# Five layer-norm boundaries: the next stage's first slab multiplied block by block, the slabs after it copied later on ScalarE

## The chip, the cores and the metric

The kernel runs on one core of a Trainium2 chip. The metric is the device time of one execution in microseconds (us). TensorE multiplies matrices, VectorE and ScalarE work on elements, GpSimd does a few small operations, and SyncE issues most transfers. The time before is the median of three runs, 965.1 us (963.51 to 965.26).

## The reference

Three transformer blocks in a row on one sequence of 256 positions and 1024 features, all in float32. Cut to what matters:

```python
# block 1
x = layer_norm(2**.25 * x + concat(stick_breaking_attention, memory_attention) @ w_out)
x = layer_norm(2**.25 * x + square(relu(x @ w_up)) @ w_down)         # 4096 wide
# block 2, layer 0
x = layer_norm(4**.25 * x + mla_mixer(x))     # low-rank q and kv, 8 heads with rotary parts
x = layer_norm(4**.25 * x + conv_ffn(x))      # (silu(g) * a) @ w_down, a and g by a 3-tap convolution
# block 2, layer 1
x = layer_norm(4**.25 * x + hyena_mixer(x))   # gated long convolutions through Fourier transforms
x = layer_norm(4**.25 * x + conv_ffn(x))
```

There are six layer norms. Five of them are followed by another stage; these five places are called boundaries here, numbered in order of time: into the first feed-forward network (FF1), into the latent attention (MLA), into the first convolution FFN, into Hyena, into the second convolution FFN.

## The kernel before, in words

**Numbers in two parts.** To reach float32 accuracy with the fast reduced type (F32R), each operand is split in a high part (a copy on ScalarE, line 67) and a low part (source minus high on VectorE, line 68). A product is three matmuls: high x high, low x high, high x low.

**Slabs.** Weights come from memory in slabs of 128 x 1024 (512 KB). `weights()` takes one of three raw buffers (`wraw`), loads it through SyncE's queue (line 82), and splits it into one of five pairs `whi`, `wlo` (pool `wspl`). A raw buffer is free again when the low part is done.

**Activations.** `x` is kept feature by feature: 8 tiles of 128 features, high and low, 256 positions in two blocks of 128 rows. `gemm_b` (line 102) multiplies a slab by x over all 256 positions, 24 matmuls of 256 columns; `gemm_wide` (lines 110 and 112), used in FF1, takes high and low x side by side, 8 matmuls of 512 columns and 8 of 256.

**A boundary** is written in `Down.end`. The down projection's last four slabs are kept back (`tail`), and in program order there follow: the tail of block 0 (12 x 2 matmuls of 512 columns); `ln_block(0)`, the norm of rows 0 to 127; the loads of the next stage's four first slabs (`w_up_f` and the like); the tail of block 1; `first_mm(0)`, 24 matmuls of 512 columns (line 199) that use block 0 of x as weights and give the next stage's first 512 outputs, position by position, copied to `utok` by ScalarE (line 201); `ln_block(1)`; `first_mm(1)`.

`ln_block` runs lines 159 to 170 on VectorE (one power on GpSimd, line 165), then eight 128x128 transposes on TensorE (line 178, tile `ln_t`), four to a bank, and splits each bank into x: high on ScalarE, low on VectorE. After the boundary the stage begins with its next slab, called the lead slab here: `ff1_mm(4)` in FF1, `c_mm(4)` in MLA, `mm(0)` in the convolution FFNs, `hy_mm(4)` in Hyena. Then come transposes of `utok` (line 209, tile `f4t`) and further slabs.

**Order.** The framework orders each engine's instructions when the program is built: of those it takes to be ready by its own estimate, the one that stands first in the program goes first. `tc.issue_after(ins)` adds one rule: what the block issues on the engine of `ins` goes behind `ins` in that engine's order. Before, it is used with `norm["inst"]`, the last VectorE instruction of the norm: `ln_block(1)` goes behind block 0's, and the low parts of the six slabs after a boundary (`norm["after"] = 6`) go behind block 1's. Their high copies on ScalarE have no such rule.

**Positions.** `rope_tables`, called in FF1 at `i == 3`, loads the positions and a small table through SyncE's queue, and VectorE and ScalarE make sine and cosine from them for the MLA stage.

Of the kernel before, what the change touches and what calls it, by code (L numbers as in the profile page):

```python
# [9 lines left out]
F32 = mybir.dt.float32  # L10
F32R = mybir.dt.float32r
# [32 lines left out]
def block_kernel(ctx, tc, A, out, taps=None):  # L44
# [21 lines left out]
    def split(hi, lo, src):  # L66
        nc.scalar.activation(hi, src, AF.Copy)  # L67
        nc.vector.tensor_tensor(lo, src, hi.bitcast(F32), op=ALU.subtract)  # L68
# [7 lines left out]
    def weights(ap, dst=None, dma=False):  # L76


        n = ap.shape[-1]
        raw = raw_tile()  # L80
        hi, lo = dst or [wspl.tile([P, 1024], F32R, name=t, tag=t) for t in ("whi", "wlo")]
        norm["load"] = nc.sync.dma_start(raw[:, :n], ap)
        if dma:
            nc.scalar.activation(hi[:, :n], raw[:, :n], AF.Copy)
            nc.scalar.activation(lo[:, :n], raw[:, :n], AF.Copy, scale=-1.0)
            nc.gpsimd.dma_start(lo[:, :n], ap, accum_op=ALU.add)
            return hi, lo
        with ExitStack() as es:
            if norm["after"] > 0:
                norm["after"] -= 1  # L90
                es.enter_context(tc.issue_after(norm["inst"].ins))
            split(hi[:, :n], lo[:, :n], raw[:, :n])
        return hi, lo
# [59 lines left out]
    def ln_block(b, acc, x, gb, alpha, last):  # L153
# [15 lines left out]
        for h, sl in enumerate(halves):  # L169
            norm["inst"] = nc.vector.scalar_tensor_tensor(s[:, sl], s[:, sl], rs, bb[:, sl],  # L170
                                                          op0=ALU.mult, op1=ALU.add)
            if last:
                nc.sync.dma_start(out[b * P:(b + 1) * P, sl], s[:, sl])
                continue
            ps = bank("ln_t")
            for k in range(4):
                kk = 4 * h + k
                nc.tensor.transpose(ps[:, k * P:(k + 1) * P], s[:, kk * P:(kk + 1) * P], ident)
            pv = ps.rearrange("p (k t) -> p k t", k=4)
            kb = (slice(None), slice(4 * h, 4 * h + 4), slice(b * P, (b + 1) * P))  # L180
            split(x[0][kb], x[1][kb], pv)
# [6 lines left out]
    def first_mm(b, x, ws, utok):  # L188
# [12 lines left out]
        nc.scalar.activation(utok[:, b, :], ps, AF.Copy)  # L201

# [11 lines left out]
    class Down:  # L214
# [24 lines left out]
        def end(self, gb, alpha, first, room=None):  # L239
            last = first is None  # L240
            x = utok = ws = None
# [5 lines left out]
            if not last:  # L247
                room = room or [None] * 4
                ws = [weights(first[i], room[i]) for i in range(4)]
            self.tail(1)  # L250
            if not last:
                first_mm(0, x, ws, utok)
            with tc.issue_after(norm["inst"].ins):
                ln_block(1, self.acc, x, gb, alpha, last)
            if not last:
                first_mm(1, x, ws, utok)
                norm["after"] = 6
            return x, utok
# [259 lines left out]
    x, utok = dn.end(gb, ALPHA_1, A["w_up_f"], spare(p1, F4_TAGS))  # L518
# [32 lines left out]
    def rope_tables():  # L551
        posi = p2.tile([P, S], I32, name="posi")
        pp = A["positions"]
        nc.sync.dma_start(posi, bass.AP(tensor=pp.tensor, offset=pp.offset, ap=[[0, P], [1, S]]))
        invf = p2.tile([P, 2], F32, name="invf")
        nc.sync.dma_start(invf, A["c_rope"])
# [40 lines left out]
    ready = [ff1_act(ff1_mm(4))]  # L597
# [12 lines left out]
    x, utok = dn.end(gb, ALPHA_1, A["mla_w_in_f"], spare(p2, F4_TAGS))  # L610
# [35 lines left out]
    c4 = c_mm(4)  # L646
# [131 lines left out]
    x, utok = dn.end(gb, ALPHA_2, A["ffn_w_up_f"][0], spare(p3, F4_TAGS))  # L778
# [88 lines left out]
    def conv_ffn(layer, x, utok, nxt, side):  # L867
        with ExitStack() as es:
# [28 lines left out]
            ready = [up(2)]  # L897
# [9 lines left out]
            return dn.end(gb, ALPHA_2, nxt)  # L907

    x, utok = conv_ffn(0, x, utok, A["hy_w_in_f"], hyena_filter)
# [137 lines left out]
    va = [hy_mm(4)]  # L1047
# [44 lines left out]
    x, utok = dn.end(gb, ALPHA_2, A["ffn_w_up_f"][1], [(room[:, i, 0], room[:, i, 1]) for i in range(4)])  # L1092
# [3 lines left out]
    conv_ffn(1, x, utok, None, None)  # L1096
# [117 lines left out]
```

## Time and profile before

| | before |
|---|---|
| median of three runs | 965.1 us |
| the profiled execution's own time | 964.65 us |
| its span (first to last instruction) | 962.9 us |
| granted TensorE clock, mean over the span | 0.992 |
| busy share TensorE / VectorE / ScalarE / GpSimd | 97% / 79% / 56% / 7% |
| bytes moved by transfers | 173.83 MB, mean 181 GB/s |

A row of the timeline gives start, duration, engine, line, operation, tiles (out<-in), shape and count; like instructions that follow each other are merged, so the duration of a merged row runs from the first one's start to the last one's end. In square brackets stands how long the engine was idle before, and who ended that. PE is TensorE, PEld its weight loads, DVE VectorE, ACT ScalarE, POOL GpSimd, SP SyncE; a "q" behind the name is the engine's sequencer. Matmuls overlap, so a row's mean duration is longer than the distance from one to the next. A row of a stretch (windows) gives its start and end, length, busy time and count of each engine, granted clock, transfer share and GB/s.

### The profile page before, as it was taken

Reading aid. Unit: us, or ns where it says so; the run is one execution under the profiler, and the core shown is the slowest. Engines: PE = TensorE matmul, PEld = TensorE weight load, DVE = VectorE, ACT = ScalarE, POOL = GpSimd, SP = SyncE. Lnnn points to the kernel's source line nnn. Section 1 sums busy time; section 2 is a strip of 40 time slices with the busy share of each in tenths; the row PEclk is TensorE's granted clock in tenths of the full one; section 3 lists DMA queues with packets and bytes.
Section 4 is the critical chain, followed back from the end, with each engine's and each line's share of the span. In section 5 each row is a group of like instructions: output and inputs, shape, how many; then the busy total and the mean of one; then the engine's idle time right before and its main releaser. Section 6 shows DMA issues by size and latency. Waiting matters only on the chain.

```text
span 962.9 us, 15208 instructions
## 1 busy us (share of the span) xinstructions
PE 932.9 (97%) x5808; PEld 823.7 (86%) x5808; DVE 761.1 (79%) x1201; ACT 539.9 (56%) x878; POOL 64.0 (7%) x61
## 2 busy tenths in 40 slices
PE   9999999999999999999999999998989999999996
PEld 6889788888887898788899999888978799999995
DVE  6887679777667879779889788889779878777776
ACT  4676636454445577556666566445675355555551
POOL 0000000000000010011312211001210000000000
PEclk9999999999999999999999999999989999999999
DMA  7764536655665443576555556436995565555551
GB/s 248 261 198 132 166 117 223 204 175 181 192 193 193 160 126 109 176 248 220 184 170 177 176 182 198 153 98 159 262 242 144 173 231 184 181 192 185 186 177 44
DMA packets 51082, 173.83 MB, mean 181 GB/s; under 512 B 6236, under 2 KB 7101, under 8 KB 50881
## 3 DMA queue, kind: packets, MB, share of 16 engines
q1 hardware_dynamic: 48656, 164.34, 52.6%
q0 software_dynamic: 2352, 8.52, 4.6%
q8 instruction: 46, 0.75, 0.3%
q14 instruction: 28, 0.22, 0.1%
HBM read 171.13 MB, written 1.05 MB: 179 GB/s over the span
## 4 chain that ended last, share of the span: by engine, by line
PE 75%; DVE 11%; DMA 7%; ACT 4%; issue 2%; SPq 0%; DVEq 0%; ACTq 0%; POOLq 0%
PE up L102 23%; PE acc L116 9%; PE acc L117 9%; PE acc L118 9%; PE up L110 5%; PE f L199 5%; DVE wlo L68 3%; PE up L112 3%; PE proj L102 2%; DMA wraw<-w_v 1%; ACT whi L67 1%; DMA wraw<-hy_w_in 1%; DMA wraw<-ffn_w_up_f 1%; PE hin L102 1%; DMA wraw<-w_qk 1%
## 5 line engine op out<-in xcount | busy, mean ns | idle before, releaser
L68 DVE TENSOR_TENSOR wlo<-wraw,whi 128x1024 fp32r<-128x1024 f32 (+1 forms) x255 | 310.4, 1220 | 78.4 <-ACT whi L67 77.5
L67 ACT ACTIVATE whi<-wraw 128x1024 fp32r<-128x1024 f32 (+1 forms) x255 | 265.2, 1044 | 128.1 <-PE acc L117 45.8
L102 PE MATMUL up<-x,whi 128*128 128x256 f32 x1280 | 173.7, 283 | 2.0 <-DVE t L790 2.0
L102 PEld LDWEIGHTS up<-x,whi 128*128 128x128 f32 x1280 | 164.8, 191 | 6.2 <-ACT whi L67 2.1
L118 PE MATMUL acc<-wlo,hh 128*128 128x512 f32 x304 | 119.9, 396 | 0.0
L116 PE MATMUL acc<-whi,hh 128*128 128x512 f32 x304 | 119.9, 396 | 0.0
L117 PE MATMUL acc<-whi,hl 128*128 128x512 f32 x304 | 119.9, 395 | 0.0
L102 PE MATMUL up<-x,wlo 128*128 128x256 f32 x640 | 89.8, 283 | 0.0
L787 ACT ACTIVATE t<-up,wc 128x256 f32<-128x256 f32 x80 | 37.7, 473 | 91.8 <-PE up L102 89.0
L102 PEld LDWEIGHTS up<-x,wlo 128*128 128x128 f32 x640 | 82.4, 192 | 0.0
L788 DVE SCALAR_TENSOR_TENSOR t<-up,wc,t 128x255 f32<-128x255 f32 x80 | 38.2, 479 | 46.3 <-ACT t L787 46.0
L118 PEld LDWEIGHTS acc<-wlo,hh 128*128 128x128 f32 x304 | 57.1, 188 | 13.5
L116 PEld LDWEIGHTS acc<-whi,hh 128*128 128x128 f32 x304 | 57.4, 189 | 11.3 <-ACT hh L67 0.5
L117 PEld LDWEIGHTS acc<-whi,hl 128*128 128x128 f32 x304 | 57.0, 188 | 11.0 <-DVE hl L68 0.3
L110 PE MATMUL up<-x,whi 128*128 128x512 f32 x224 | 56.6, 395 | 0.0
L165 POOL TENSOR_TENSOR ln_rs<-ln_rs,mhalf 128x1 f32<-128x1 f32 x12 | 11.5, 958 | 646.3 <-DVE ln_rs L164 646.3
L110 PEld LDWEIGHTS up<-x,whi 128*128 128x128 f32 x224 | 41.8, 188 | 10.6 <-issue 1.1
L102 PE MATMUL hin<-x,whi 128*128 128x256 f32 x320 | 46.7, 292 | 0.0
L102 PEld LDWEIGHTS hin<-x,whi 128*128 128x128 f32 x320 | 42.7, 199 | 0.3
L790 DVE SCALAR_TENSOR_TENSOR t<-up,wc,t 128x255 f32<-128x255 f32 x80 | 38.3, 480 | 2.1
L67 ACT ACTIVATE hh<-h 128x256 fp32r<-128x256 f32 x32 | 13.1, 415 | 39.1 <-DVE h L544 38.0
L112 PEld LDWEIGHTS up<-x,wlo 128*128 128x128 f32 x224 | 30.6, 190 | 2.3
(404 smaller groups left out, 1665.2 us busy)
## 6 DMA issues: line engine op xcount, KB each, us to landing
wraw<-ffn_w_up SPq DMA_DIRECT2D x80, 512.0 KB, 4.2
wraw<-ffn_w_down SPq DMA_DIRECT2D x44, 512.0 KB, 3.7
wraw<-w_down SPq DMA_DIRECT2D x32, 512.0 KB, 3.5
wraw<-w_up SPq DMA_DIRECT2D x28, 512.0 KB, 4.3
wraw<-hy_w_in SPq DMA_DIRECT2D x20, 512.0 KB, 5.1
wraw<-w_qk SPq DMA_DIRECT2D x14, 512.0 KB, 4.5
wlo<-hy_w_in POOLq DMA_DIRECT2D x11, 512.0 KB, 9.4
wraw<-w_out SPq DMA_DIRECT2D x8, 512.0 KB, 3.4
```

Of the source, the lines that this page charges most:

```text
L67: nc.scalar.activation(hi, src, AF.Copy)
L68: nc.vector.tensor_tensor(lo, src, hi.bitcast(F32), op=ALU.subtract)
L102: nc.tensor.matmul(ps, a[:, off + k * P:off + (k + 1) * P], m[:, k, :], start=i == 0, stop=i == len(seq) - 1)
L110: nc.tensor.matmul(ps, wh[:, k * P:(k + 1) * P], xx[:, k], start=k == 0, stop=False)
L112: nc.tensor.matmul(ps[:, :S], wl[:, k * P:(k + 1) * P], xh[:, k, :], start=False, stop=k == KT - 1)
L116: nc.tensor.matmul(ps, ah, mh, start=start, stop=False)
L117: nc.tensor.matmul(ps, al, mh, start=False, stop=False)
L118: nc.tensor.matmul(ps, ah, ml, start=False, stop=stop)
L199: nc.tensor.matmul(ps, x[xi][:, k, tb], ws[k // 2][wi][:, o:o + 512], start=i == 0, stop=i == len(seq) - 1)
L787: norm["act"] = nc.scalar.activation(dst, ps, AF.Copy, scale=w3[:, 1:2])
L788: nc.vector.scalar_tensor_tensor(dst[:, 1:], ps[:, :S - 1], w3[:, 0:1], dst[:, 1:], op0=ALU.mult, op1=ALU.add)
L790: norm["dve"] = nc.vector.scalar_tensor_tensor(dst[:, :S - 1], ps[:, 1:S], w3[:, 2:3], dst[:, :S - 1], op0=ALU.mult, op1=ALU.add)
```

## The change

The lead slab moves into `Down.end`. Its load and its high copy stand behind the four first slabs; the high copy goes behind block 0's last high split of x on ScalarE (`norm["x"]`). `lead_mm(0)`, 16 matmuls of 128 columns (high weights by high and by low x of block 0), stands behind `first_mm(0)` and ahead of `ln_block(1)`. Behind `first_mm(1)` stand the low part (VectorE, after block 1's norm), `lead_mm(1)`, 16 more, and 8 matmuls of 256 columns with the low weights. The results gather in one PSUM bank, an accumulator bank of the down projection where the first slabs have room of their own (boundaries 1, 2, 3 and 5), else a bank of the common pool. In FF1 the lead is no longer in the wide form, so its activation takes the Relu path of `ff1_act`.

The next five slabs' high copies on ScalarE now go behind block 1's last high split of x, as their low parts already went behind block 1's norm. The positions and their table are loaded through GpSimd's queue.

```diff
     def split(hi, lo, src):
-        nc.scalar.activation(hi, src, AF.Copy)
-        nc.vector.tensor_tensor(lo, src, hi.bitcast(F32), op=ALU.subtract)
+        return (nc.scalar.activation(hi, src, AF.Copy),
+                nc.vector.tensor_tensor(lo, src, hi.bitcast(F32), op=ALU.subtract))
...
             if norm["after"] > 0:
                 norm["after"] -= 1
                 es.enter_context(tc.issue_after(norm["inst"].ins))
+                es.enter_context(tc.issue_after(norm["x"].ins))
             split(hi[:, :n], lo[:, :n], raw[:, :n])
...
-            split(x[0][kb], x[1][kb], pv)
+            norm["x"] = split(x[0][kb], x[1][kb], pv)[0]
...
+    def lead_mm(ps, b, x, hi):
+
+        tb = slice(b * P, (b + 1) * P)
+        for j in range(2):
+            for k in range(KT):
+                nc.tensor.matmul(ps[:, tb], hi[:, k * P:(k + 1) * P], x[j][:, k, tb],
+                                 start=(b, j, k) == (0, 0, 0), stop=False)
...
-        def end(self, gb, alpha, first, room=None):
+        def end(self, gb, alpha, first, lead=None, room=None):
...
                 ws = [weights(first[i], room[i]) for i in range(4)]
+                raw = raw_tile()
+                lw = [wspl.tile([P, 1024], F32R, name=t, tag=t) for t in ("whi", "wlo")]
+                nc.sync.dma_start(raw, lead)
+                with tc.issue_after(norm["x"].ins):
+                    nc.scalar.activation(lw[0], raw, AF.Copy)
             self.tail(1)
             if not last:
+                ps = bank("lead") if room[0] is None else acc_bank(0, 0, "lead")
                 first_mm(0, x, ws, utok)
+                lead_mm(ps, 0, x, lw[0])
             with tc.issue_after(norm["inst"].ins):
                 ln_block(1, self.acc, x, gb, alpha, last)
             if not last:
                 first_mm(1, x, ws, utok)
-                norm["after"] = 6
-            return x, utok
+                with tc.issue_after(norm["inst"].ins):
+                    nc.vector.tensor_tensor(lw[1], raw, lw[0].bitcast(F32), op=ALU.subtract)
+                lead_mm(ps, 1, x, lw[0])
+                ps = ps[:, :S]
+                for k in range(KT):
+                    nc.tensor.matmul(ps, lw[1][:, k * P:(k + 1) * P], x[0][:, k, :], start=False, stop=k == KT - 1)
+                norm["after"] = 5
+            return x, utok, ps
...
-        nc.sync.dma_start(posi, bass.AP(tensor=pp.tensor, offset=pp.offset, ap=[[0, P], [1, S]]))
+        nc.gpsimd.dma_start(posi, bass.AP(tensor=pp.tensor, offset=pp.offset, ap=[[0, P], [1, S]]))
         invf = p2.tile([P, 2], F32, name="invf")
-        nc.sync.dma_start(invf, A["c_rope"])
+        nc.gpsimd.dma_start(invf, A["c_rope"])
...
-    ready = [ff1_act(ff1_mm(4))]
+    ready = [ff1_act(lead)]
...
-    c4 = c_mm(4)
...
-            ready = [up(2)]
+            ready = [act(2, [lead, mm(1)])]
...
-    va = [hy_mm(4)]
+    va = [lead]
```

The calls of `dn.end` pass the lead slab (`A["w_up"][0]`, `A["mla_w_in"][0]`, `A["ffn_w_up"][0, 0]`, `A["hy_w_in"][0]`, `A["ffn_w_up"][1, 0]`) and hand its result on.

More of the change, by code (lines that the diff above doesn't have):

```diff
@@ L237, in tail @@
                     gemm_a(self.acc, b, h, act, w, False, i == len(self.pend) - 1)
-        def end(self, gb, alpha, first, room=None):
+        def end(self, gb, alpha, first, lead=None, room=None):
             last = first is None
-            x = utok = ws = None
+            x = utok = ws = lw = ps = None
             self.tail(0)
@@ L517, in block_kernel @@
         u_dn(k)
-    x, utok = dn.end(gb, ALPHA_1, A["w_up_f"], spare(p1, F4_TAGS))
+    x, utok, lead = dn.end(gb, ALPHA_1, A["w_up_f"], A["w_up"][0], spare(p1, F4_TAGS))
     ph.close()
@@ L609, in block_kernel @@
             next(mlp, None)
-    x, utok = dn.end(gb, ALPHA_1, A["mla_w_in_f"], spare(p2, F4_TAGS))
+    x, utok, c4 = dn.end(gb, ALPHA_1, A["mla_w_in_f"], A["mla_w_in"][0], spare(p2, F4_TAGS))
     ph.close()
@@ L777, in block_kernel @@
         u_wo(k)
-    x, utok = dn.end(gb, ALPHA_2, A["ffn_w_up_f"][0], spare(p3, F4_TAGS))
+    x, utok, lead = dn.end(gb, ALPHA_2, A["ffn_w_up_f"][0], A["ffn_w_up"][0, 0], spare(p3, F4_TAGS))
     ph.close()
@@ L864, in hyena_filter, with conv_ffn @@
         return steps + [(load_dft, "c_inv1"), (load_dft, "c_inv2")]
-    def conv_ffn(layer, x, utok, nxt, side):
+    def conv_ffn(layer, x, utok, lead, nxt, nxt_lead, side):
         with ExitStack() as es:
@@ L906, in conv_ffn @@
                         f(*a)
-            return dn.end(gb, ALPHA_2, nxt)
-    x, utok = conv_ffn(0, x, utok, A["hy_w_in_f"], hyena_filter)
+            return dn.end(gb, ALPHA_2, nxt, nxt_lead)
+    x, utok, lead = conv_ffn(0, x, utok, lead, A["hy_w_in_f"], A["hy_w_in"][0], hyena_filter)
     tap("t_l0")
@@ L1091, in block_kernel @@
     room = keep.tile([P, 4, 2, D], F32R, name="Kf", tag="Kf")
-    x, utok = dn.end(gb, ALPHA_2, A["ffn_w_up_f"][1], [(room[:, i, 0], room[:, i, 1]) for i in range(4)])
+    x, utok, lead = dn.end(gb, ALPHA_2, A["ffn_w_up_f"][1], A["ffn_w_up"][1, 0], [(room[:, i, 0], room[:, i, 1]) for i in range(4)])
     ph.close()
     tap("t_hy")
-    conv_ffn(1, x, utok, None, None)
+    conv_ffn(1, x, utok, lead, None, None, None)
 def _tiles(w):
```

## The prediction

> **What bounds the kernel now.** I read the page's busy shares and chain first, then TensorE's waits, then the five layer-norm boundaries stretch by stretch, and last their timelines. Durations come from the profiled execution, which took 964.65 us (span 962.9); the median of the runs shown, 965.1, is 0.45 us above it.
>
> ```profile
> span 962.9 us, 15208 instructions
> PE 932.9 (97%) x5808; PEld 823.7 (86%) x5808; DVE 761.1 (79%) x1201; ACT 539.9 (56%) x878; POOL 64.0 (7%) x61
> PE 75%; DVE 11%; DMA 7%; ACT 4%; issue 2%; SPq 0%; DVEq 0%; ACTq 0%; POOLq 0%
> ```
>
> TensorE is busy 97% of the span and holds three quarters of the chain. So work added to TensorE is time added, unless it falls into one of TensorE's idle stretches, and the question is how much idle time the boundaries have. TensorE's waits by releaser (total us, times, longest):
>
> ```profile
> PE hin L102 <- DMA wlo<-hy_w_in: 3.7, 4, 1.8
> PE y L116 <- DVE g L790: 2.7, 2, 2.2
> PE hyt L935 <- DVE u L790: 2.6, 1, 2.6
> ...
> PE up L102 <- DVE t L790: 2.0, 2, 1.8
> ...
> PE f L199 <- ACT x L67: 0.9, 3, 0.3
> ```
>
> The last row is the wait that the change aims at: first_mm (L199) for the copy of the normalised rows. It is 0.9 us in the whole program. The other rows lie inside later stages (Hyena, first convolution FFN). The five boundaries, each from the end of the down projection's tail into the lead slab (window, length, then busy us of TensorE, weight loads, VectorE, ScalarE, GpSimd):
>
> ```profile
> 128.40:144.20 15.80, 15.50 (x76) 12.71 (x75) 12.20 (x17) 5.08 (x8) 0.99 (x1) 1.00 0.36 124
> 314.00:330.00 16.00, 15.94 (x85) 13.02 (x84) 13.58 (x23) 6.08 (x15) 0.92 (x1) 1.00 0.33 105
> 406.50:422.20 15.70, 15.40 (x82) 12.97 (x81) 12.39 (x17) 4.39 (x7) 0.93 (x1) 1.00 0.43 130
> 619.00:637.00 18.00, 16.10 (x85) 12.90 (x84) 13.95 (x20) 7.45 (x10) 0.99 (x1) 1.00 0.40 124
> 757.00:781.00 24.00, 23.64 (x123) 19.37 (x123) 19.46 (x30) 9.23 (x13) 1.91 (x2) 1.00 0.43 154
> ```
>
> TensorE is idle 0.30, 0.06, 0.30, 1.90 and 0.36 us there: only the fourth boundary (into Hyena) has a hole worth filling. The third (into the first convolution FFN) stands for the others; TensorE, then ScalarE, then VectorE:
>
> ```profile
> 410.49 2.03 PE L199 MATMUL f<-f4h,x 128*128 128x512 f32 x8
> 412.36 1.03 PE L178 MATMUL ln_t<-ident,xt 128*128 128x128 f32 x8
> 413.70 1.21 PE L199 MATMUL f<-f4h,x 128*128 128x512 f32 x4 [0.30 <-ACT x L67]
> ...
> 419.32 1.12 PE L102 MATMUL up<-x,whi 128*128 128x256 f32 x8
> ...
> 421.24 2.08 PE L102 MATMUL up<-x,whi 128*128 128x256 f32 x16
> ```
>
> ```profile
> 412.56 0.60 ACT L201 ACTIVATE utok<-f 128x512 f32<-128x512 f32 x1 [5.85 <-PE f L199]
> 413.05 1.08 ACT L67 ACTIVATE x<-ln_t 128x512 fp32r<-128x512 f32 x2
> ```
>
> ```profile
> 410.53 1.41 DVE L170 SCALAR_TENSOR_TENSOR xt<-xt,ln_rs,ln_b 128x512 f32<-128x512 f32 x2
> ```
>
> Block 1's norm ends on VectorE at 411.94, before first_mm(0) ends, so the transposes start at 412.36 with no wait. They are issued by 412.36 + 8 x 0.109 = 413.23; block 1's first matmul starts at 413.70, a hole of 0.47 us.
>
> **Paces.** A merged row gives the pace as (its time less one duration) / (count less one). 128x512: (2.03 - 0.40) / 7 = 0.233 us. 128x256: (2.08 - 0.28) / 15 = 0.120. 128x128 transposes: (1.03 - 0.27) / 7 = 0.109. (0.40, 0.28 and 0.27 are the single durations of those shapes.)
>
> **The lead slab's matmuls.** Before, the lead slab costs 24 matmuls of 256 columns, 24 x 0.120 = 2.88 us; at the first boundary it is the wide form (8 of 512, 8 of 256), and takes 144.02 - 141.21 = 2.81:
>
> ```profile
> 141.21 2.01 PE L110 MATMUL up<-x,whi 128*128 128x512 f32 x8
> ...
> 144.02 1.03 PE L209 MATMUL f4t<-ident,utok 128*128 128x128 f32 x8
> ```
>
> After, it is 2 x 16 of 128 columns and 8 of 256: half the columns in each of the 32, but each loads its own 128x128 weights. No row of before has such a matmul on the reduced type. From below, weights with a single moving column; from above, plain f32 at 256 columns:
>
> ```profile
> 338.07 0.51 PE L667 MATMUL ss<-ones,sq 128*128 128x1 f32 x4
> ```
>
> ```profile
> 394.12 1.13 PE L760 MATMUL o<-sm_pt,v_mla 128*128 128x256 f32 x4 [0.74 <-ACT sm_pt L294]
> ```
>
> These give (0.51 - 0.25) / 3 = 0.087 and (1.13 - 0.39) / 3 = 0.248. I take 0.109, the transposes: nearest in shape (128 weight columns, 128 moving), and the first row says that the weights alone cost nearly that. The 0.120 of the 256-column rows is the likely slow end. New lead: 32 x 0.109 + 8 x 0.120 = 4.45 us. That is +1.64 at the first boundary and +1.57 at each of the second, third and fifth.
>
> The row for weights says a 128-column matmul can't halve the 256-column one. [...]
>
> **Fourth boundary.** TensorE, ScalarE and VectorE:
>
> ```profile
> 623.06 2.00 PE L199 MATMUL f<-whi,x 128*128 128x512 f32 x8
> 625.74 0.44 PE L209 MATMUL f4t<-ident,utok 128*128 128x128 f32 x2 [0.69 <-ACT utok L201]
> 627.30 1.38 PE L178 MATMUL ln_t<-ident,xt 128*128 128x128 f32 x8 [1.12 <-DVE xt L170]
> ```
>
> ```profile
> 622.58 1.06 ACT L67 ACTIVATE whi<-wraw 128x1024 fp32r<-128x1024 f32 x1 [2.44 <-DMA wraw<-hy_w_in]
> ```
>
> ```profile
> 626.50 1.41 DVE L170 SCALAR_TENSOR_TENSOR xt<-xt,ln_rs,ln_b 128x512 f32<-128x512 f32 x2
> ```
>
> first_mm(0) is issued by 623.06 + 8 x 0.23 = 624.9, and the transposes wait for the norm until 627.30: 2.4 us with 0.2 of work in them. The lead's high copy ends at 623.6, so lead_mm(0), 16 x 0.109 = 1.74, fits in wholly. What is left after block 1 is 1.74 + 0.96 = 2.70 against 2.88: -0.18. The late thing is then still block 1's norm.
>
> **Order at the other four.** lead_mm(0) stands ahead of ln_block(1) in the program, and the transposes are ready when first_mm(0) ends, so it goes ahead of them: it pushes transposes, copy and first_mm(1) back by 1.74 us and fills no hole. What it does save: utok's copy is off ScalarE by then. The first four transposes end at 412.36 + 3 x 0.109 + 0.27 = 412.96, and the copy started at 413.05: 0.09 saved at boundaries one and three, about 0.10 at the fifth, where the rows wait for VectorE instead, nothing at the second: -0.28. The fifth boundary, where the transposes run into VectorE's end but the hole is the same, 771.57 - (770.23 + 8 x 0.109) = 0.47:
>
> ```profile
> 770.23 1.33 PE L178 MATMUL ln_t<-ident,xt 128*128 128x128 f32 x8
> 771.57 5.87 PE L199 MATMUL f<-Kf,x 128*128 128x512 f32 x24
> ```
>
> **Copies held back on ScalarE.** Five slabs' high copies now wait for block 1's high split. At the first boundary (ScalarE, VectorE):
>
> ```profile
> 125.43 2.01 ACT L67 ACTIVATE whi<-wraw 128x1024 fp32r<-128x1024 f32 x2 [5.14 <-PE acc L117]
> ...
> 134.89 1.08 ACT L67 ACTIVATE x<-ln_t 128x512 fp32r<-128x512 f32 x2
> ```
>
> ```profile
> 133.56 2.35 DVE L68 TENSOR_TENSOR wlo<-wraw,whi 128x1024 fp32r<-128x1024 f32 x2
> ```
>
> The two copies of 125.43 move behind the split, which ends near 137.6 (135.97 + 1.74 - 0.09): the second slab is copied by 138.7 and subtracted by 139.9. It is needed after the lead and the eight transposes of 144.02, at about 146.4: cost nothing, slack 6 us. Its raw buffer is freed 4 to 5 us later than before (133.56 + 2.35 = 135.9), so the load into it lands near 139.9 + 3.5 = 143.4 instead of 139.4, and three slabs of 2.8 us each stand before its use:
>
> ```profile
> wraw<-w_down SPq DMA_DIRECT2D x32, 512.0 KB, 3.5
> ```
>
> Queued behind the held copies on ScalarE: utok's copy and the activations, all after first_mm(1). Without that slack a slab costs 1.06 + 1.22 us of ScalarE and VectorE time in the open. The lead's high copy waits for block 0's split, over 5 us before its use. The low part after the norm was so before. The loads keep their order on SyncE.
>
> **Positions on GpSimd's queue.** Two small DMAs leave SyncE's queue, for a queue with nothing in it (GpSimd):
>
> ```profile
> 310.89 0.99 POOL L165 TENSOR_TENSOR ln_rs<-ln_rs,mhalf 128x1 f32<-128x1 f32 x1 [178.82 <-DVE ln_rs L164]
> ```
>
> They can only go earlier; GpSimd's next work is 179 us away. VectorE loses a wait under a TensorE-bound stage: 0. If they landed late, VectorE's conversion would hold the splits queued behind it, with several slabs ahead as cover. The lead's activation in the first FFN (Relu and one multiply instead of three operations) and the accumulator bank borrowed for the lead: 0, both end before that bank's first use.
>
> **Sum.** 1.64 + 3 x 1.57 - 0.18 - 0.28 = +5.9 us: 964.65 becomes 970.5, on the scale of the median 971.0. In general, with p the pace of a 128-column matmul, the sum is 144p - 9.8 us. The unknown ends: p = 0.087 gives +2.7; p = 0.120 gives +7.5; p = 0.248 gives about +28 (there lead_mm(0) no longer fits into the fourth hole).
>
> **Rivals.**
> - *The 128-column matmul takes its streaming time alone* (not slower). Weights load under the matmul before, and p is half of 0.120, 0.060: 144 x 0.060 - 9.8 = -1.2, 964. It decides from p below 0.08, where the sum is under 0.2%. For it: at 256 columns loads hide. Against: the 0.087 of the single-column row. [...] Chance 0.14.
> - *The reduced type falls to the plain f32 pace below 256 columns*: p = 0.248, about 993. No row excludes it. Chance 0.07.
> - *The next stage absorbs part.* In the first convolution FFN TensorE waits 1.8 us for VectorE (row "up"). If VectorE's backlog isn't pushed back too, that takes the 1.57 of this boundary: +4.3, 969.4. Against: VectorE's work there begins with the lead's activation, so it moves as well. Chance 0.15.
> - *The order changes in Hyena* (faster). The build order around the four waits of 3.7, 2.7, 2.6 and 2.0, together 11.0 us, could come out otherwise; it must return over 7.8 of them to be a gain, and if all went, 960. Chance 0.10, more than half of it faster.
>
> **Numbers.** My forecast of 971.0 has 0.54 (its own range 969.5 to 973). A change under 0.2% (1.9 us) is about what a measurement of this kernel can't tell from none. Faster 0.08 (most of the last rival), within 0.2% 0.17 (the streaming rival and bits of the last two), slower 0.75. The range 963.5 to 975 holds all but the fast half of the last rival, the f32 rival and the tails.
>
> **What would show it.** Matmuls of the lead at 128 columns with a pace near 0.109; 88 more matmuls (4 x 16 + 24); at boundaries one, two, three and five lead_mm(0) ahead of the transposes, TensorE still idle 0.3 to 0.5 before first_mm(1), and first_mm(1) later by 1.6 to 1.9; at the fourth no idle stretch of over 0.7; no new wait of TensorE for a whi or wlo in the ten us behind a boundary. The prediction fails if the 128-column pace is not 0.10 to 0.12, if the transposes go ahead of lead_mm(0) and it fills the holes, or if waits inside Hyena or the first convolution FFN move by microseconds.

## The result, and the profile after

The change made the kernel slower: 992.5 us (median of four runs, 991.58 to 993.38) against 964.65 us (median of four runs of the kernel before, measured beside it), a ratio of 1.029 (95% interval 1.0272 to 1.0308), about 28 us. The forecast was 971.0. The profiled execution took 991.76 us, with a span of 990.0 us, 27.1 above the span before. From the page of the kernel after: the span, the engines' busy time, and the chain by engine.

```profile
span 990.0 us, 15384 instructions
PE 946.0 (96%) x5896; PEld 836.6 (85%) x5896; DVE 761.2 (77%) x1200; ACT 538.0 (54%) x878; POOL 66.3 (7%) x63
PE 71%; DMA 11%; DVE 9%; ACT 5%; issue 4%; SPq 0%; DVEq 0%; POOL 0%; ACTq 0%; POOLq 0%
```

TensorE has the 88 more matmuls that were forecast (5896 against 5808). But its share of the chain fell from 75% to 71%, and that of transfers rose from 7% to 11%: the time went into waits. TensorE's waits after, by releaser (total us, times, longest):

```profile
PE hin L103 <- DMA wlo<-hy_w_in: 8.8, 3, 5.6
PE acc L117 <- ACT hh L67: 6.1, 1, 6.1
...
PE acc L118 <- DVE hl L68: 2.0, 1, 2.0
...
PE f L200 <- ACT x L67: 1.0, 4, 0.3
```

The last row is the wait at which the change aimed: 0.9 us before, 1.0 after. The first is Hyena's, 3.7 before. The next two did not exist.

**Where it went, stage by stage.** I cut each trace where TensorE starts block 1's transposes (`ln_t`) at each boundary; for the kernel before these starts are 134.20, 320.01, 412.36, 627.30 and 770.23 us. This gives six stretches. "Forecast" takes the prediction's own terms apart in the same way: lead_mm(0) of a boundary falls into the stretch that ends there, lead_mm(1) and the low part into the next.

| stretch (us) | to 1st boundary | FF1 | MLA | conv FFN 0 | Hyena | conv FFN 1 |
|---|---|---|---|---|---|---|
| before | 134.20 | 185.81 | 92.35 | 214.94 | 142.93 | 192.66 |
| after | 134.97 | 195.15 | 94.49 | 222.27 | 150.99 | 192.11 |
| change | +0.8 | +9.3 | +2.1 | +7.3 | +8.1 | -0.6 |
| forecast | +1.7 | +1.5 | +1.6 | -0.3 | +1.6 | -0.3 |

Three stretches miss: FF1 by 7.8 us, the first convolution FFN by 7.6, Hyena by 6.5. The other three are within 1 us. These are stretches of one execution each; how much such a stretch moves by itself is said below the table of the experiments, and the experiments have to show the causes.

**The boundaries themselves went as forecast.** TensorE's timeline of the kernel after, at the third boundary:

```profile
421.05 2.00 PE L200 MATMUL f<-f4h,x 128*128 128x512 f32 x8
422.88 1.90 PE L209 MATMUL lead<-x,whi 128*128 128x128 f32 x16
424.62 1.06 PE L179 MATMUL ln_t<-ident,xt 128*128 128x128 f32 x8
425.93 1.19 PE L200 MATMUL f<-f4h,x 128*128 128x512 f32 x4 [0.25 <-ACT x L67]
...
431.53 1.90 PE L209 MATMUL lead<-x,whi 128*128 128x128 f32 x16
433.27 1.16 PE L278 MATMUL lead<-x,wlo 128*128 128x256 f32 x8
```

The lead's pace is (1.90 - 0.27) / 15 = 0.109 us, the value taken. lead_mm(0) stands ahead of the transposes and fills nothing: the hole before first_mm(1) is still there, 425.93 - (424.62 + 8 x 0.109) = 0.44 us. At the fourth boundary it does fill the hole, and what is late there is the norm, by 0.58 us:

```profile
644.41 1.90 PE L209 MATMUL lead<-x,whi 128*128 128x128 f32 x16
646.89 1.29 PE L179 MATMUL ln_t<-ident,xt 128*128 128x128 f32 x8 [0.58 <-DVE xt L171]
```

**FF1: the conversion of the positions.** GpSimd, VectorE, ScalarE and TensorE of the kernel after, just behind the first boundary:

```profile
142.76 0.74 POOL L576 DMA_DIRECT2D posi<-positions  x1 [11.72 <-ACT utok L202]
```

```profile
150.17 0.29 DVE L580 CAST ang<-posi 128x256 f32<-128x256 int32 x1 [5.21 <-DMA posi<-positions]
...
153.71 0.75 DVE L562 TENSOR_TENSOR h<-h 128x256 f32<-128x256 f32 x2
```

```profile
154.16 0.75 ACT L67 ACTIVATE hh<-h 128x256 fp32r<-128x256 f32 x2 [7.73 <-DVE h L562]
```

```profile
147.42 1.11 PE L113 MATMUL up<-x,wlo 128*128 128x256 f32 x8
154.63 0.79 PE L117 MATMUL acc<-whi,hh 128*128 128x512 f32 x1 [6.10 <-ACT hh L67]
```

Read them backwards. TensorE waits 6.10 us for the split of the first activation (`hh`), ScalarE for VectorE's square of it (`h`), and VectorE for the positions, which land 7.3 us after GpSimd issues them. What the squares read was there by 146.44, when ScalarE's part of the activation ended; VectorE began them at 153.71, behind the conversion and the work on the angles. In the kernel before, the conversion stood behind the squares and splits of the first activations and waited 0.57 us:

```profile
149.51 0.75 DVE L540 TENSOR_TENSOR h<-h 128x256 f32<-128x256 f32 x2
150.41 0.76 DVE L68 TENSOR_TENSOR hl<-h,hh 128x256 fp32r<-128x256 f32 x2
151.74 0.30 DVE L558 CAST ang<-posi 128x256 f32<-128x256 int32 x1 [0.57 <-DMA posi<-positions]
```

The transfer did land earlier, at 142.76 + 7.3 = 150.1 against 151.7. But the builder of the order put the conversion ahead of the squares, so it must have taken the transfer to be there earlier still (its estimates are not on record). All that VectorE had to do for TensorE's next matmuls stood behind the conversion.

**Hyena: the low copy of slab 12.** Slabs named in `HY_DMA` get their low part in two steps: ScalarE writes the negated high part (line 85, called the low copy here), and a transfer on GpSimd's queue adds the weights from memory to it. ScalarE, GpSimd and TensorE of the kernel after:

```profile
670.28 1.05 ACT L84 ACTIVATE whi<-wraw 128x1024 fp32r<-128x1024 f32 x1
...
682.78 0.47 ACT L808 ACTIVATE u<-hin,ws 128x256 f32<-128x256 f32 x1 [2.69 <-PE hin L103]
683.22 0.60 ACT L67 ACTIVATE zh<-hyt 128x512 fp32r<-128x512 f32 x1
683.71 1.05 ACT L85 ACTIVATE wlo<-wraw 128x1024 fp32r<-128x1024 f32 x1
```

```profile
685.07 0.87 POOL L86 DMA_DIRECT2D wlo<-hy_w_in  x1 [20.42 <-ACT wlo L85]
```

```profile
694.90 2.08 PE L103 MATMUL hin<-x,wlo 128*128 128x256 f32 x8 [5.56 <-DMA wlo<-hy_w_in]
```

The low copy stands 13.4 us behind the high copy of the same slab, behind activations that wait for TensorE. In the kernel before, the two were 6.3 us apart, and TensorE waited 1.47 us for the transfer; its ScalarE, then TensorE:

```profile
654.58 1.06 ACT L84 ACTIVATE whi<-wraw 128x1024 fp32r<-128x1024 f32 x1 [1.37 <-DMA wraw<-hy_w_in]
...
660.87 1.04 ACT L85 ACTIVATE wlo<-wraw 128x1024 fp32r<-128x1024 f32 x1
```

```profile
670.01 1.22 PE L102 MATMUL hin<-x,wlo 128*128 128x256 f32 x8 [1.47 <-DMA wlo<-hy_w_in]
```

The likely reason is that the lead at this boundary changed which instructions the builder saw as ready, and so this place in its list; no_lead4 below tests it.

### The profile page after: what moved, and what is told of

It reads as the page before. It is cut to its first block, busy times and chain, and to the rows that moved or that the text cites. A ratio compares the mean times of both kernels' runs of the same rounds, so it can differ in the third digit from the quotient of the medians.

```text
span 990.0 us, 15384 instructions
## 1 busy us (share of the span) xinstructions
PE 946.0 (96%) x5896; PEld 836.6 (85%) x5896; DVE 761.2 (77%) x1200; ACT 538.0 (54%) x878; POOL 66.3 (7%) x63
## 4 chain that ended last, share of the span: by engine, by line
PE 71%; DMA 11%; DVE 9%; ACT 5%; issue 4%; SPq 0%; DVEq 0%; POOL 0%; ACTq 0%; POOLq 0%
PE up L103 20%; PE acc L117 8%; PE acc L118 8%; PE acc L119 8%; PE f L200 5%; PE up L111 5%; DVE wlo L68 3%; PE up L113 2%; DMA wraw<-hy_w_o 2%; PE proj L103 2%; ACT whi L67 1%; PE lead L209 1%; DMA wraw<-w_qk 1%; DMA wraw<-ffn_w_up 1%; PE hin L103 1%
## 5 line engine op out<-in xcount | busy, mean ns | idle before, releaser
L68 DVE TENSOR_TENSOR wlo<-wraw,whi 128x1024 fp32r<-128x1024 f32 (+1 forms) x250 | 303.8, 1219 | 89.8 <-ACT whi L67 88.6
L67 ACT ACTIVATE whi<-wraw 128x1024 fp32r<-128x1024 f32 (+1 forms) x250 | 259.4, 1044 | 109.2 <-PE acc L118 31.6
L103 PE MATMUL up<-x,whi 128*128 128x256 f32 x1248 | 170.1, 283 | 0.7 <-DVE t L811 0.7
L103 PEld LDWEIGHTS up<-x,whi 128*128 128x128 f32 x1248 | 161.4, 192 | 4.6 <-issue 0.7
L103 PEld LDWEIGHTS up<-x,wlo 128*128 128x128 f32 x624 | 81.2, 193 | 0.0
L809 DVE SCALAR_TENSOR_TENSOR t<-up,wc,t 128x255 f32<-128x255 f32 x78 | 37.2, 479 | 45.4 <-ACT t L808 45.2
L111 PE MATMUL up<-x,whi 128*128 128x512 f32 x216 | 54.6, 394 | 0.0
L111 PEld LDWEIGHTS up<-x,whi 128*128 128x128 f32 x216 | 40.2, 188 | 10.3 <-issue 1.1
L811 DVE SCALAR_TENSOR_TENSOR t<-up,wc,t 128x255 f32<-128x255 f32 x78 | 37.3, 480 | 2.1
L103 PE MATMUL hin<-x,wlo 128*128 128x256 f32 x152 | 23.4, 299 | 9.0 <-DMA wlo<-hy_w_in 8.8
```

The lines of the kernel that those rows point to most:

```text
L67: return (nc.scalar.activation(hi, src, AF.Copy), nc.vector.tensor_tensor(lo, src, hi.bitcast(F32), op=ALU.subtract))
L103: nc.tensor.matmul(ps, a[:, off + k * P:off + (k + 1) * P], m[:, k, :], start=i == 0, stop=i == len(seq) - 1)
L111: nc.tensor.matmul(ps, wh[:, k * P:(k + 1) * P], xx[:, k], start=k == 0, stop=False)
L809: nc.vector.scalar_tensor_tensor(dst[:, 1:], ps[:, :S - 1], w3[:, 0:1], dst[:, 1:], op0=ALU.mult, op1=ALU.add)
L811: norm["dve"] = nc.vector.scalar_tensor_tensor(dst[:, :S - 1], ps[:, 1:S], w3[:, 2:3], dst[:, :S - 1], op0=ALU.mult, op1=ALU.add)
```

## The experiments

Medians, ratios to the kernel before measured beside them (95% interval), and the stretches of one profiled execution each (conv 0 is the first convolution FFN):

| kernel | median us | ratio | FF1 | MLA | conv 0 | Hyena |
|---|---|---|---|---|---|---|
| pos_only | 969.53 | 1.0055 (1.0032 to 1.0077) | 189.96 | 92.20 | 216.55 | 140.37 |
| hold_only | 972.2 | 1.0072 (1.0048 to 1.0095) | 185.50 | 94.04 | 220.25 | 140.49 |
| lead_only | 984.88 | 1.0198 (1.0164 to 1.0233) | 191.52 | 94.82 | 218.96 | 146.72 |
| pos_sync | 983.2 | 1.0193 (1.0152 to 1.0233) | 186.86 | 94.31 | 220.00 | 152.19 |
| pos_late | 979.9 | 1.0141 (1.0102 to 1.0181) | 186.71 | 93.97 | 219.86 | 153.02 |
| no_hold3 | 981.01 | 1.0151 (1.0122 to 1.0181) | 187.25 | 94.71 | 219.70 | 151.74 |
| no_lead4 | 974.75 | 1.0095 (1.0066 to 1.0125) | 187.18 | 94.22 | 220.72 | 143.57 |
| early12 | 980.15 | 1.0143 (1.0114 to 1.0173) | 187.02 | 93.99 | 222.95 | 145.71 |
| fixed | 972.79 | 1.0072 (1.0051 to 1.0094) | 186.74 | 94.48 | 216.99 | 146.90 |
| fixed_whole | 962.32 | 0.9966 (0.9951 to 0.9981) | 184.90 | 92.53 | 217.38 | 137.28 |
| before_f2 | 965.05 | 0.9992 (0.997 to 1.0013) | 185.54 | 92.49 | 214.63 | 139.86 |
| lead4_f2 | 966.61 | 1.0009 (0.999 to 1.0029) | 185.48 | 92.12 | 215.12 | 142.92 |
| before_f2e | 961.76 | 0.9949 (0.993 to 0.9969) | 185.06 | 93.10 | 215.19 | 139.43 |
| whole_nohold | 958.39 | 0.992 (0.9889 to 0.995) | 185.64 | 92.84 | 214.33 | 136.51 |

A caution for the table: a stretch is from one execution. pos_sync and early12 have the same order up to Hyena, and differ by 3.0 us in conv 0; pos_only and the kernel before have the same order in Hyena, and differ by 2.6 there. Differences under 3 us in these two stretches show nothing alone.

### The three parts of the change, one by one

pos_sync is the change without its positions part:

```diff
-        nc.gpsimd.dma_start(posi, ...)
-        nc.gpsimd.dma_start(invf, A["c_rope"])
+        nc.sync.dma_start(posi, ...)
+        nc.sync.dma_start(invf, A["c_rope"])
```

> The changed kernel with the positions and their table loaded through SyncE's queue again; all else as changed. Theory 1 (VectorE's conversion of the positions stands early in its order and waits 5.2 us for a load that lands 7.3 us after its issue on GpSimd's queue; TensorE then waits 6.1 us and restarts at a lower clock): about 7.7 us come back, near 985. Rival (the wait in the first FFN is that of the held copies and late slabs, the positions only happen to end it): stays within 2 us of 992.5.

pos_only is the kernel before with that part alone (the reverse of this diff).

> The kernel before with only the positions and their table moved to GpSimd's queue. Theory 1: the same wait appears in the first FFN, +5 to +8 us, 970 to 973. Rival (the move alone is hidden by the slabs that are ready ahead): within 1 us of before, 964 to 966.

hold_only is the kernel before with the held copies alone (six slabs behind a boundary, since there is no lead):

```diff
                 es.enter_context(tc.issue_after(norm["inst"].ins))
+                es.enter_context(tc.issue_after(norm["x"].ins))
```

> The kernel before with only the high copies of the six slabs behind a boundary held behind block 1's split on ScalarE. Theory 2 (the loss of about 15 us in the first convolution FFN and in Hyena comes from the held copies: raw buffers come free later and the loads behind them too): 975 to 980. Rival (it comes from the lead slab taken by blocks, which moves the build order of all engines in those stages): 964 to 967 here.

lead_only is the change without that added line and with the positions on SyncE.

> The changed kernel without the hold on the following slabs' copies and with the positions on SyncE: only the lead slab by blocks, its own high copy behind block 0's split. Theory 2: only the extra matmuls remain, +5.9 us, 970 to 972. Rival (the build order of later stages is moved by the lead slab): 978 to 986.

Measured: without the positions part 983.2, with it alone 969.5 (5 us, just under the times expected), so it costs 5 to 9 us, and FF1 shows where: 195.15 falls to 186.86. The held copies alone cost 7 us, most of it in conv 0 (+5.3); that lies between what theory 2 asked for (975 to 980) and what its rival did (964 to 967). The lead alone costs 19 us, against 5.9 by its matmuls: there theory 2 failed, and the rival, that the lead moves the order of later stages, came out. The parts do not add up by stretch: in conv 0 the hold alone costs 5.3, the lead alone 4.0, both together 5.1. That fits a stage whose slack can be lost only once, which no run tests by itself.

lead_only also shows why the copies were held. At the first boundary ScalarE's next slab copy stood ahead of the rows' split and waited for its load; ScalarE and TensorE of lead_only:

```profile
137.94 1.06 ACT L67 ACTIVATE whi<-wraw 128x1024 fp32r<-128x1024 f32 x1 [3.33 <-DMA wraw<-w_up]
138.90 1.07 ACT L67 ACTIVATE x<-ln_t 128x512 fp32r<-128x512 f32 x2
```

```profile
139.54 1.18 PE L199 MATMUL f<-f4h,x 128*128 128x512 f32 x4 [2.92 <-ACT x L67]
```

### pos_late: the queue, or the place in VectorE's list

```diff
         ang = p2.tile([P, S], F32, name="ang")
-        nc.vector.tensor_copy(ang, posi)
+        with tc.issue_after(norm["lo"].ins):      # the last split's subtraction
+            nc.vector.tensor_copy(ang, posi)
```

> The changed kernel whole, positions still on GpSimd's queue, but VectorE's conversion of the positions is put behind the last split's subtraction that the program has issued by then. Theory (the queue is harmless, the early place of the conversion in VectorE's order is what stopped the first FFN): the FF1 segment falls from 195.15 to 186.5-188 us, the 6.1 us wait of acc L117 for ScalarE's hh is gone, and the time is that of the kernel with SyncE's positions, 982 to 985. Rival (the queue itself, a transfer from GpSimd disturbing the slab loads or landing late): FF1 stays at 193 to 196, the time at 990 to 993.

Measured: FF1 falls from 195.15 to 186.71, the total is 979.9 (975.3 to 983.01), 2 us below what was expected, and about what the kernel with SyncE's positions takes. Positions still come by GpSimd's queue, the conversion runs at 161.33 without a wait, and TensorE no longer stops. VectorE and TensorE of pos_late:

```profile
161.33 0.28 DVE L583 CAST ang<-posi 128x256 f32<-128x256 int32 x1
```

```profile
148.00 1.11 PE L115 MATMUL up<-x,wlo 128*128 128x256 f32 x8
148.95 0.40 PE L119 MATMUL acc<-whi,hh 128*128 128x512 f32 x1
```

So the queue is harmless; the place in the list cost the 8 us.

### no_lead4 and early12: Hyena

no_lead4 is pos_sync with the fourth boundary as it was (`dn.end(..., None)` there, six slabs held, `va = [hy_mm(4)]`).

> The change with SyncE's positions, and the fourth boundary (into Hyena) as before: no lead slab in the down projection's end there, its six slabs held instead. Theory (the lead at this boundary changes the order that the builder writes for Hyena, and slab 12's low copy goes 13 us behind its high copy): the 5 us wait of TensorE for a wlo by accumulating transfer goes, the Hyena segment falls from 152.2 to 140-145, the total to 972 to 976. Rival (Hyena's loss comes from the five other changes ahead of it or from held copies): Hyena stays above 149, total near 983.

early12 is pos_sync with three slabs written earlier in Hyena:

```diff
     ga = pair_mm(8)
+    for nt in (10, 11, 12):
+        early[nt] = hy_w(nt)                  # the slab's weights(...); hy_mm takes it from here
     v_fin(z1, 1, 6, vb)
```

> The change with SyncE's positions and the lead at all five boundaries, but in Hyena the loads and splits of slabs 10, 11 and 12 are written ahead of v_fin(z1, 1, 6, vb), so that ScalarE's low copy of slab 12 stands right behind its high copy and ahead of two activations that wait for TensorE; the matmuls stay where they are in the program. Theory (the low copy's place in ScalarE's order is the cause of the 5 us wait): that wait falls under 2 us, Hyena from 152.2 to 144-148, total 976 to 980. Rival (the slab is late for its buffer or its transfer, whatever ScalarE's order): the wait stays at 4 to 6 us or moves to the next slab, Hyena above 150.

Measured: Hyena 143.57 without the lead at this boundary, 145.71 with the lead and the early slabs, against 152.19. TensorE's whole wait for accumulated low parts falls from 7.4 us to 1.9 and 1.6. ScalarE and GpSimd of early12 show the low copy 1.3 us behind its high copy:

```profile
664.25 1.06 ACT L84 ACTIVATE whi<-wraw 128x1024 fp32r<-128x1024 f32 x1 [1.01 <-issue]
665.57 1.05 ACT L85 ACTIVATE wlo<-wraw 128x1024 fp32r<-128x1024 f32 x1
```

```profile
666.92 0.88 POOL L86 DMA_DIRECT2D wlo<-hy_w_in  x1 [8.88 <-PE X L119]
```

So the order is the cause, and the lead at the fourth boundary is what changed it. early12 moves the loads of three slabs too, not the low copy alone; but in the kernel after slab 12 lay in its raw buffer by 670.28, when its high copy began, so it was not the load that held the low copy back until 683.71. early12's total of 980.15 is just above what was expected; its conv 0 came out 3 us longer than that of pos_sync.

### no_hold3: the first convolution FFN

```diff
-                es.enter_context(tc.issue_after(norm["x"].ins))
+                if norm["n"] != 3:                # boundaries counted in norm["n"]
+                    es.enter_context(tc.issue_after(norm["x"].ins))
```

> The change with SyncE's positions, and without the hold of ScalarE's copies at the third boundary only (into the first convolution FFN). Theory (held copies free the raw buffers later, and the loads of that stage come late): the conv0 segment falls from 220.0 by 2 to 5 us and the total by as much, to 978 to 981. Rival (the lead slab itself costs that stage its slack, the copies are hidden): conv0 stays within 1 us of 220, the total near 983. The kernel with the lead and no hold anywhere had 218.96 there, so 1 us less is the least that the theory can live with.

Measured: conv 0 219.70, no change, so by its own terms the theory failed. The traces show two different stops. With the hold (pos_sync), a slab's load is issued at 425.35, behind the two loads of the next norm's parameters (424.45 and 424.83), and takes 7.9 us; in the kernel before, one is issued ahead of those two (419.21 against 419.75). ScalarE waits 2.77 us for that load, with the first activations behind it in its list, and GpSimd's work on the Hyena filter (`f_wpm`) then falls onto their splits. hold_only has the same wait of ScalarE, 2.69 us, and the same pair of stops of TensorE, 1.50 and 1.84 us. ScalarE, GpSimd, VectorE and TensorE of pos_sync:

```profile
433.29 1.06 ACT L67 ACTIVATE whi<-wraw 128x1024 fp32r<-128x1024 f32 x1 [2.77 <-DMA wraw<-ffn_w_up]
```

```profile
436.90 2.94 POOL L848 TENSOR_TENSOR f_wpm<-f_wfb 128x512 f32<-128x512 f32 x2 [23.30 <-DVE t L912]
```

```profile
436.99 1.73 DVE L68 TENSOR_TENSOR c_fwdl<-wraw,c_fwdh 128x512 fp32r<-128x512 f32 x1
438.64 0.47 DVE L809 SCALAR_TENSOR_TENSOR t<-f4t,wc,t 128x255 f32<-128x255 f32 x1
439.04 1.09 DVE L68 TENSOR_TENSOR hl<-t,hh 128x256 fp32r<-128x256 f32 x1
```

```profile
437.72 0.47 PE L117 MATMUL acc<-whi,hh 128*128 128x512 f32 x1 [1.10 <-issue]
440.18 0.80 PE L118 MATMUL acc<-whi,hl 128*128 128x512 f32 x1 [1.98 <-DVE hl L68]
```

Without the hold, the builder put ScalarE's split of `f_wpm` ahead of the stage's own activations, and ScalarE stood for 8.25 us. ScalarE and TensorE of no_hold3:

```profile
435.74 0.63 ACT L67 ACTIVATE f_wh<-f_wpm 128x512 fp32r<-128x512 f32 x1 [8.25 <-POOL f_wpm L850]
436.27 0.46 ACT L810 ACTIVATE t<-up,wc 128x256 f32<-128x256 f32 x1
```

```profile
438.80 2.05 PE L104 MATMUL up<-x,whi 128*128 128x256 f32 x8 [5.18 <-DVE t L813]
```

So I formed another theory: the filter's side work is part of both stops.

### fixed and fixed_whole: all three orders put right, then the lead whole

fixed is the change whole, with pos_late's and early12's edits and the filter's side work later:

```diff
-                if i:
-                    for f, *a in todo[(i - 1) * per:i * per]:
+                if i > 2:
+                    for f, *a in todo[(i - 3) * per:(i - 2) * per]:
...
+            with ExitStack() as es:               # in load(): its loads and splits
+                for k in ("load", "act", "dve"):  # behind the last load and convolution so far
+                    es.enter_context(tc.issue_after(norm[k].ins))
```

> The changed kernel whole (lead slabs, held copies, positions on GpSimd's queue) with three places of the order put right: VectorE's conversion of the positions behind the last split issued by then; Hyena's slabs 10 to 12 loaded and split ahead of v_fin(z1, 1, 6, vb); in the first convolution FFN the side work of the Hyena filter (loads and splits) two tiles later and behind that tile's last convolution on ScalarE and VectorE and the last load on SyncE. Theory (all that the change costs beyond the lead's matmuls is order): FF1 near 187, conv0 216 to 219, Hyena 144 to 147, total 970 to 975. Rival (the held copies and late loads cost conv0 its 5 us whatever the filter does): conv0 stays at 220 to 222 and the total at 976 to 980.

fixed_whole is the same with 24 matmuls of 256 columns behind first_mm(1) in place of lead_mm(0) and lead_mm(1).

> As the kernel with the three places of the order put right, but each lead slab is multiplied whole behind first_mm(1), 24 matmuls of 256 columns, instead of block by block. Theory (a 128-column matmul takes 0.109 us, nearly as long as one of 256): TensorE works 16 x 0.109 + 16 x 0.109 - 16 x 0.120 = 1.57 us less at each boundary; the time falls by 1.57 at boundaries one, two, three and five and by nothing or less at the fourth, where the first part filled a hole: 5 to 7 us below its neighbour. Rival (the split by blocks hides the wait for the rows' split, worth what it costs): within 2 us of its neighbour.

Measured: fixed takes 972.79, inside what was expected, and so are its stretches. That is +7.1 us on the kernel before beside it (965.73), with an interval of +4.9 to +9.1; the forecast was +5.9. The three edits return 20 of the 28 us. But two of them are edits that the kernel before could have as well, and with them it is before_f2e below, 961.76: against that one, fixed costs 11.0 us, most of it in Hyena (146.90 against 139.43). So the order in Hyena was mended only in part, and the nearness of 7.1 to 5.9 is partly luck. conv 0 is 216.99, 2.4 above before_f2; alone that is too little to tell, but of the kernels with the later filter the two that hold copies have 216.99 and 217.38 there, and the four without a hold 214.33 to 215.19, so the hold keeps 2 to 3 us. fixed_whole takes 962.32: the blocks cost 10.5 us, more than the 5 to 7 expected. FF1 (-1.84) and MLA (-1.95) are near the 1.6 of the matmuls, but Hyena falls by 9.6 where the matmuls explain 1.6; the rest is not explained by them, and was not taken apart.

### before_f2, lead4_f2, before_f2e, whole_nohold: what is worth keeping

before_f2 is the kernel before with the later filter work alone.

> The kernel before, with only the Hyena filter's side work two tiles later, as above. Theory (GpSimd's and ScalarE's filter work collides with the first tiles of the first convolution FFN in the kernel before too: 2.2 us of TensorE's waiting at 27 us into that stage): conv0 from 214.9 to 212-214, total 962 to 964.5. Rival (that wait is VectorE's backlog from the boundary alone): conv0 within 1 us of 214.9, or later by what the filter's end now costs, total 964 to 968.

lead4_f2 adds the lead by blocks at the fourth boundary alone and early12's edit; nothing is held.

> The kernel just named, with the lead slab by blocks at the fourth boundary alone (there the norm of block 1 leaves TensorE idle for 1.9 us), and Hyena's slabs 10 to 12 loaded early. No held copies, positions on SyncE. Theory (there, and only there, the first part of the lead falls into a hole): 0 to 2 us below its neighbour. Rival (Hyena's order takes back more than the hole gives, as the 145.7 us of Hyena with the early slabs against 142.9 before say): 1 to 4 us above it.

before_f2e adds early12's edit alone to before_f2.

> The kernel before with the filter's side work two tiles later and Hyena's slabs 10 to 12 loaded and split early; no lead, no held copies. The kernel with the lead multiplied whole had Hyena at 137.3 us, 9.6 below its neighbour by blocks, where the matmuls' own price is 1.7. Theory A (the early slabs give Hyena a better order, and only the blocks of the lead had spoilt it): Hyena falls from 139.9-142.9 to 136-139, total 958 to 963. Theory B (the good order comes with the lead's early load and its place in the down projection's end): Hyena stays at 140 to 145, total 963 to 967.

whole_nohold is fixed_whole without the line that holds the copies, and with the positions on SyncE.

> The kernel with the lead multiplied whole and the orders put right, but with nothing held on ScalarE and the positions on SyncE. Theory (the held copies cost the first convolution FFN its remaining 2.5 us, 217.4 against 214.6, and give nothing elsewhere): conv0 214 to 216, FF1 near 185, the total 1 to 3 us below its neighbour. Rival (without the hold the copies stand ahead of the rows' split on ScalarE, and the wait of first_mm(1), 3.7 us where the lead ran without hold, comes back): total 1 to 6 us above it.

Measured: the later filter alone changes nothing that can be told (ratio 0.9992). Its conv 0 is 214.63 where the theory asked for 212 to 214, so that theory failed, though the 1.82 us wait of TensorE that ended at 439.59 is gone.

The early slabs are the next step from there: before_f2e has a ratio of 0.9949, some 3 us below before_f2. Theory A asked for a Hyena of 136 to 139; it came out at 139.43 against 139.86 for before_f2, so the total fits theory A, but the profiled executions do not show where the 3 us come from.

The lead by blocks gains nothing even at the boundary with a hole. lead4_f2 is 1.6 us above before_f2, as the rival had it. The nearer neighbour is before_f2e, which differs from it by the lead alone: against that one it is 4.9 us slower (966.61 against 961.76, ratios 1.0009 and 0.9949, intervals apart).

whole_nohold is the best, 958.39 us, a ratio of 0.992 (0.9889 to 0.995): it beats the kernel before by about 7 us and the changed one by 34. Its conv 0 is 214.33, 3.0 below fixed_whole, as expected (the total is 3.9 below, a little more than expected), and the wait for the rows' split did not come back (0.9 us in all). The early slabs without any lead already give 4 of the 7 us (before_f2e), and the intervals of these two kernels overlap, so what the lead's early load adds is not shown; its Hyena, 136.51, is 2.9 below that of before_f2e, on the border of what one execution tells.

## Why the prediction was wrong, point by point

- **Direction and the matmuls' term: right.** The pace was 0.109 as taken, the 88 matmuls came, lead_mm(0) went ahead of the transposes and the holes stayed; FF1 and MLA give 1.84 and 1.95 us back when the lead is multiplied whole. The whole, 28 us, is nearly five times the 5.9 of this term: what failed is what the prediction put at nothing. The rival that gave about 993 (plain f32 pace, 0.248) hit the number by accident: the rows of the lead have 0.109.
- **Positions on GpSimd's queue, put at 0: the first failed step, 8 us.** "They can only go earlier" held for the transfer. The sentence behind it, that a late landing would only hold up splits with "several slabs ahead as cover", named the wrong work. Behind the conversion stood the squares of the first activations, and TensorE had one `up` slab to do before it needed them.
- **Copies held back on ScalarE, put at nothing with 6 us of slack: the second, 3 to 5 us in the first convolution FFN** (hold_only +5.3, fixed_whole against whole_nohold 3.0). The step was worked out at the first boundary, where it holds (FF1 of hold_only is 185.50). It was not worked out at the third, where a slab's load goes behind the norm's parameters and the filter's work falls onto the first splits. In the changed kernel, taking the hold off at that boundary alone returned nothing (219.70): the lead brought another stop of TensorE, 5.18 us, in its place.
- **The order in Hyena: the third, about 6.5 us.** It was seen as a rival, but with a gain as its main outcome and a 0.10 chance; the row "hin <- DMA wlo" (3.7 us), one of the four that it hung on, went to 8.8. The fourth boundary's own term, -0.18, went the same way: lead_mm(0) did fill the hole there, and yet the lead at that boundary alone costs 4.9 us (lead4_f2 against before_f2e).
- **The range.** Every cost of order was bounded at zero on one side, since the trace of before showed slack. A slack that is read from one built order did not carry over to the next one: three of the six stretches lost 6 to 8 us more than forecast, and the lead alone, without the two other parts, cost 19 us where its matmuls explain 5.9 (lead_only).
- The last condition of failure that the prediction named, waits inside Hyena or the first convolution FFN that move by microseconds, is what happened; FF1, the dearest, was not on that list.

## What to carry to other kernels

When a program orders each engine's list at build time from estimates, an edit that is free by its own work can still move another instruction ahead of a wait; look for instructions whose input comes late (here a small load, for which VectorE stood 5.21 us in the kernel after; a GpSimd result, ScalarE 8.25 in no_hold3; an accumulating transfer, TensorE 5.56 in the kernel after) and ask what stands behind them on their engine. Such places can be found in the timeline of a run and mended with an edit of the order each: three of them gave 20 us back here. Measure such an edit on the kernel before as well, since part of what it gives may have nothing to do with the change. Splitting a 256-column matmul in two of 128 columns nearly doubled its price here (0.109 against 0.120 us each), so it can pay only in an idle stretch longer than itself, and here it did not pay even there.

## What the runs showed of the hardware

**Behind some waits TensorE ran at half clock.** Stretches of the kernel after, around the 6.10 us wait; the number behind the five engines' busy times and counts is the granted clock (1.00 is full):

```profile
148.50:154.60 6.10, 0.03 (x1) 0.00 (x0) 4.22 (x13) 0.44 (x2) 0.00 (x0) 0.69 0.36 144
154.63:157.49 2.86, 2.86 (x6) 2.11 (x7) 2.86 (x8) 2.84 (x5) 0.00 (x0) 0.50 0.65 204
157.80:160.00 2.20, 2.20 (x11) 1.83 (x10) 2.16 (x8) 2.04 (x5) 0.00 (x0) 1.00 0.61 187
```

Behind the wait, matmuls of 512 columns start 0.43 us apart instead of 0.23 for 2.9 us. How long a wait must be for this is not told by its length alone. In the kernel before, half clock followed a wait of 2.56 us (656.58 to 659.14). Of two waits of 1.82 us it followed the one that ended at 700.10, and not the one that ended at 439.59:

```profile
659.14:662.60 3.46, 3.46 (x19) 3.46 (x19) 3.46 (x6) 2.37 (x3) 0.39 (x1) 0.60 0.01 2
439.59:443.00 3.41, 3.41 (x27) 3.32 (x28) 3.41 (x5) 0.41 (x3) 3.06 (x2) 1.00 0.34 135
700.79:704.20 3.41, 3.41 (x15) 2.69 (x13) 1.73 (x3) 3.41 (x7) 0.87 (x1) 0.50 1.07 280
```

In the kernel after, it did not follow a wait of 2.94 us (660.95 to 663.89, clock 1.00 to 667.30), and it did follow one of 1.64 us (492.57 to 494.21, clock 0.50 from 495.56 to 498.97). The stretches of half clock start on a grid: those of the kernel before at 38.60, 659.83, 700.79 and 707.61, that is 621.23, 40.96 and 6.82 us apart, or 182, 12 and 2 times 3.413 (40.96 / 12), and each lasts 3.41 us (6.83 behind the two longest waits of the kernel after, 6.10 and 5.56). So where a wait falls on that grid may decide; the runs do not settle the rule.

Over the span the clock lost (1 - 0.985) x 990.0 = 14.9 us after and (1 - 0.992) x 962.9 = 7.7 before. Part of that lies inside the waits themselves and behind TensorE's last matmul, where it costs nothing; counted where TensorE was busy, half clock took 11.1 us after and 6.7 before. So by these two counts I estimate that some 4 of the 27 us are this echo of the waits: each stretch counted, four before and six after, starts inside a wait of TensorE of 1.48 us or more, or less than 1.5 us behind one.

**Beside GpSimd's elementwise work some of VectorE's operations took longer.** The subtraction `c_fwdl` took 1.73 us beside `f_wpm` in pos_sync, and 0.69 us in the kernel before, where it ended ahead of it. In the kernel before, the product `t<-t,t` took 1.51 us beside `f_wpm` (433.31) and 0.43 without (428.83). Not every operation did: `t<-f4t,wc,t` took 0.47 us beside `f_wpm` in pos_sync (438.64) and 0.47 without (440.05). The subtraction in the kernel before:

```profile
429.62 0.69 DVE L68 TENSOR_TENSOR c_fwdl<-wraw,c_fwdh 128x512 fp32r<-128x512 f32 x1 [0.37 <-ACT c_fwdh L67]
```

**The small load of the positions took 7.3 us from issue to landing on GpSimd's queue** in the kernel after, and on SyncE's 5.7 in the kernel before and 6.0 in pos_sync. With one such transfer in each, these runs do not show that one queue is slower for it.
